# Turning the second attention group's queries by a transposing transfer in a two-layer encoder, and the keys' split at normal priority

## The chip, the cores and the metric

The kernel runs on one core of a Trainium2 chip, in one launch. The metric is the device time of the launch in microseconds. A core has a matrix engine (TensorE, PE in the profile, with its weight loads as PEld), VectorE (DVE), ScalarE (ACT), GpSimd (POOL) and SyncE (SP), whose queue here issues nearly all transfers. Every engine works through its own instructions in order and waits on semaphores for the others.

## The reference

Two layers of an encoder on 256 tokens with width 1024. Each layer normalizes its input, multiplies it by one wide matrix, feeds two branches with the parts, merges them, and goes on to a feed-forward part and an input embedding. The change lies in branch B, the attention: 8 query heads of 128, in two groups of 4, each group with one key and value head.

```python
u = rms_norm(h, g_mix_pre)
(gq, gk, gv, gg, ra_f, ra_b, aq, ak, av, gate_a, gate_b) = jnp.split(u @ w_in, offsets, axis=-1)
...
q = apply_axial_rope(rms_norm(aq.reshape(b, s, ATTN_HEADS, HEAD_DIM), g_q_norm), cos, sin)
k = apply_axial_rope(rms_norm(ak.reshape(b, s, ATTN_KV_HEADS, HEAD_DIM), g_k_norm), cos, sin)
v = av.reshape(b, s, ATTN_KV_HEADS, HEAD_DIM)
branch_b = gqa_attention(q, k, v) @ w_o_attn
...
sc = jnp.einsum('bqkgd,bskd->bkgqs', qblk, k).astype(jnp.float32) * scale
pr = jax.nn.softmax(sc, axis=-1).astype(v.dtype)
return jnp.einsum('bkgqs,bskd->bqkgd', pr, v)
```

Branch A is a gated linear attention, whose decays are built from the Abs, Exp and Ln of a projection.

## The kernel before

The 256 tokens are two halves of 128, one token in each partition. Every f32 product is made of three passes over rounded parts: each operand is split into a high part (rounded to fp32r) and a low part (the rest). `split(hi, lo, src)` does it with a cast on ACT (`nc.scalar.copy`) and a subtract on DVE, both on one line, L135 in the profile of before. Weights come by the SP queue into tiles named raw, ACT casts them to wh, DVE subtracts to wl, on the same line.

Names in the profile carry the layer and the stage: `acc_0v` is a PSUM accumulator of layer 0 in the projection of the gated branch's values, `aux_0at` a PSUM tile of the attention, `mid_0at` an on-chip tile of it, `big_0kv` the tile with the split keys and values, `mid_0rq` the rotated queries, `gqk`, `v`, `gg` the later projections, `gla` the gated branch. `acc` and `aux` share the 8 banks of PSUM, so that an accumulator can have to wait for the reader of the tile that had its bank before.

The projections are the main program. The attention and the gated branch are side tasks (`Task`), which a tick between groups of matmuls advances by a step; the `yield W[...]` say how many ticks each step waits. In this way the keys and the first group (g = 0) run in the projections kv and gqk, and the second group (g = 1) in v and gg. The build's scheduler orders each engine's instructions by priority: `tc.high_priority(n)` lets instructions go ahead of n others, and `tc.issue_after(x)` keeps them behind instruction x.

In `attend(g)`, for each half, PE turns the group's 4 heads of queries by 4 transposes (L1269) into an aux tile, and `split` takes them from there, at high priority in the first group alone. `softmax` makes the scores (matmuls on L107, `aux_0at<-big_0kv,mid_0at`), the maxima (L1230) and the exponentials (L1239); the last of these is kept in `last_exp`. `turn_p` turns the probabilities by PE (L1256) and splits them, and `passes` (L123) multiplies them by the values. `keys` turns the keys by PE (L1206) and splits them at L1209. `decays` is the gated branch's step with Abs, Exp and Ln (L1326 to L1328), read by DVE on L1329.

The kernel already has another way to turn a tile, used in the feed-forward part and for the out-gate: `turn_out` copies the f32 tile on ACT into two planes of 16-bit words (L467) and issues a transposing transfer (`dma_start_transpose`, L468) on the SP queue, and `take_in` has ACT put the turned planes together (L477) and splits the result.

Of the kernel before, what the change touches and what calls it, by code (L numbers as in the profile page):

```python
# [13 lines left out]
U16 = mybir.dt.uint16  # L14
# [4 lines left out]
P = 128  # L19
# [6 lines left out]
AHEAD, EMPTY, EMPTY_FIRST = 400, 100, 1600  # L26

WAIT, WAIT_FIRST = 6, 4

WAIT_NEXT, WAIT_IN, WAIT_H = (7, 9), ((6, 9), (6, 7)), ((3, 5), (3, 5))  # L30
WAIT_MIX = 3, 6
# [30 lines left out]
def trunk_kernel(ctx: ExitStack, tc: tile.TileContext, a: dict, out: bass.AP):  # L62
# [7 lines left out]
    nc = tc.nc  # L70
# [13 lines left out]
    def nm(s):  # L84
        uid[0] += 1
        return f"{s}_{part[0]}_{uid[0]}"
# [4 lines left out]
    def mid(dt=F32):  # L91
        return b4p.tile([P, 1024], dt, tag="mid", name=nm("mid"))
# [4 lines left out]
    def aux():  # L97
        return accp.tile([P, 512], F32, tag="acc", name=nm("aux"))

    def t512():  # L100
        return smp.tile([P, 512], F32, tag="t512", name=nm("t512"), bufs=5)

    def small(n, tag, bufs=None):
        return smp.tile([P, n], F32, tag=tag, name=nm(tag), **({"bufs": bufs} if bufs else {}))
# [10 lines left out]
    def passes(o, parts, start, stop, fresh=False, between=None, **kw):  # L115

        ps = [((xh, yh), (xh, yl), (xl, yh)) if fresh else ((xh, yh), (xl, yh), (xh, yl)) for (xh, xl), (yh, yl) in parts]  # L120
        seq = [p for t in ps for p in t[:2]] + [t[2] for t in ps]
        for n, (x, y) in enumerate(seq):
            nc.tensor.matmul(o, x, y, start=start and n == 0, stop=stop and n == len(seq) - 1, **kw)  # L123
            if between is not None and 2 * (n + 1) == len(seq):
                between()
# [7 lines left out]
    def split(hi, lo, src):  # L133

        return nc.scalar.copy(hi, src), nc.vector.tensor_tensor(out=lo, in0=src, in1=hi.bitcast(F32), op=ALU.subtract)  # L135
# [27 lines left out]
    ident = cp.tile([P, P], F32, tag="ident", name="ident")  # L163
# [204 lines left out]
    ws = Stream(4)  # L368
# [102 lines left out]
    def take_in(hi, lo, src, parts, behind=()):  # L471

        tn = hi.shape[-1]
        with ExitStack() as order:
            for x in behind:
                order.enter_context(tc.issue_after(x.ins))
            nc.scalar.copy(  # L477
                parts.bitcast(U16).rearrange("p (k t s) -> p k t s", s=2, t=tn),
                src.bitcast(U16).rearrange("p (s k t) -> p k t s", s=2, t=tn),
            )  # L480
            split(hi, lo, parts.rearrange("p (k t) -> p k t", t=tn))
# [7 lines left out]
    def inv_sqrt(t, n, mul, add, eps=None):  # L489

        with in_turn():
            if eps is None:
                nc.gpsimd.tensor_scalar(out=t, in0=t, scalar1=mul, scalar2=add, op0=ALU.mult, op1=ALU.add)
            else:
                nc.gpsimd.tensor_scalar(out=t, in0=t, scalar1=eps, scalar2=mul, op0=ALU.add, op1=ALU.mult)
        last_pow[0] = nc.gpsimd.tensor_tensor(out=t, in0=t, in1=neghalf[:, :n], op=ALU.pow)

    def split_by(hi, lo, src, r):

        nc.scalar.activation(hi, src, AF.Copy, bias=0.0, scale=r)  # L500
        nc.vector.scalar_tensor_tensor(
            out=lo, in0=src, scalar=r, in1=hi.bitcast(F32), op0=ALU.mult, op1=ALU.subtract
        )
# [43 lines left out]
    def halves(t):  # L547
        return [t[:, j * 512 : (j + 1) * 512] for j in range(2)]
# [501 lines left out]
    for l in range(DEPTH):  # L1050
# [11 lines left out]
        def rope(src, n, tabs, hf, dst):  # L1062

            ct, sn = tabs
            t2 = t512()
            hv = lambda t: t[:, : n * P].rearrange("p (h d) -> p h d", d=P)
            vmul(hv(dst), hv(src), ct[:, hf, :].unsqueeze(1).broadcast_to([P, n, P]))

            quad = lambda t: t.rearrange("p h (x y i) -> p h x y i", x=2, y=2)
            vmul(  # L1070
                quad(hv(t2)),
                quad(hv(src))[:, :, :, ::-1, :],
                quad(sn[:, hf, :].unsqueeze(1)).broadcast_to([P, n, 2, 2, 32]),
            )
            nc.vector.tensor_tensor(out=hv(dst), in0=hv(dst), in1=hv(t2), op=ALU.add)

        def head_ss(src, n, junk, ss):
            for i in range(n):
                s = slice(i * P, (i + 1) * P)
                nc.scalar.activation(junk[:, s], src[:, s], AF.Square, accum_out=ss[:, i : i + 1])  # L1080
# [28 lines left out]
        qrs, qss, ranks = [], [], []  # L1109
# [69 lines left out]
        kTh, kTl, avh, avl = (kv4[:, i * 512 : (i + 1) * 512] for i in range(4))  # L1179

        def keys(o):
            krs = []
            for hf in range(2):
                with tc.high_priority(EMPTY):
                    kr = t512()
                    ss = small(2, "kss")
                    head_ss(o[hf], 2, kr, ss)
                    inv_sqrt(ss, 2, 1.0 / P, EPS, eps[hf])
                    rope(o[hf], 2, ropes[1], hf, kr)
                    s = slice(hf * 256, (hf + 1) * 256)  # L1190
                    split_by(avh[:, s], avl[:, s], o[hf][:, 256:512], rows[hf])
                    for i in range(2):
                        s = slice(i * P, (i + 1) * P)
                        if l == 0:
                            nc.scalar.activation(kr[:, s], kr[:, s], AF.Copy, bias=0.0, scale=ss[:, i : i + 1])
                            continue
                        nc.vector.tensor_scalar(
                            out=kr[:, s], in0=kr[:, s], scalar1=ss[:, i : i + 1], scalar2=None, op0=ALU.mult
                        )
                krs.append(kr)  # L1200
            for hf in range(2):
                yield W["k"]
                ps = aux()
                for i in range(2):
                    s = slice(i * P, (i + 1) * P)
                    nc.tensor.transpose(ps[:, s], krs[hf][:, s], ident)  # L1206
                kv = lambda t: t.rearrange("p (g t) -> p g t", t=T)[:, :, hf * P : (hf + 1) * P]
                with tc.high_priority(AHEAD):
                    split(kv(kTh), kv(kTl), ps[:, 0:256].rearrange("p (g t) -> p g t", t=P))  # L1209

        keys = Task(keys(project(uT)), f"{l}kv")
        even = small(512, "rope0", 1)[:, 0:P]
        Task(spread(rho, even), f"{l}kv")
# [4 lines left out]
        last_exp = [None]  # L1218
# [32 lines left out]
        def turn_p(pr_):  # L1251
            res = []
            for s in range(2):
                ps = aux()
                for i in range(4):
                    nc.tensor.transpose(ps[:, i * P : (i + 1) * P], pr_[:, i, s * P : (s + 1) * P], ident)  # L1256
                pT = halves(mid(F32R))
                split(pT[0], pT[1], ps)
                res.append(pT)
            return res  # L1260

        def attend(g):
            qs = []
            for hf in range(2):
                yield W["q"]
                ps = aux()
                for i in range(4):
                    hd = 4 * g + i
                    nc.tensor.transpose(ps[:, i * P : (i + 1) * P], qrs[hf][:, hd * P : (hd + 1) * P], ident)  # L1269
                qh, ql = halves(mid(F32R))  # L1270
                with nullcontext() if g else tc.high_priority(AHEAD):
                    split(qh, ql, ps)
                qs.append((qh, ql, qss[hf][:, 4 * g : 4 * g + 4]))
            keys.need()
            yield W["a0"]
            prs = []
            for hf in range(2):
                prs.append(softmax(g, hf, qs[hf]))
                yield W["a1"]
            for hf in range(2):  # L1280
                pT = turn_p(prs[hf])
                yield W["a2"]
                o = aux()
                vs = [slice(s * 256 + g * P, s * 256 + (g + 1) * P) for s in range(2)]
                passes(o, [((avh[:, c], avl[:, c]), pT[s]) for s, c in enumerate(vs)], True, True)
                aT.put(o, 4 * g, 4, hf * P, P)
                yield W["a3"]

        def attention():
            for g_ in range(2):  # L1290
                part[0] = f"{l}at{g_}"
                yield from attend(g_)
# [500 lines left out]
```

## Time and profile before

| | |
|---|---|
| median of 3 runs | 905.2 us (905.08 to 906.77) |
| the profiled execution | 904.09 us |
| its span | 902.4 us |
| PE busy | 893.1 us (99%) |
| DVE busy | 789.8 us (88%) |
| ACT busy | 633.6 us (70%) |
| POOL busy | 98.1 us (11%) |

The profile is of one execution, and times in it count from the start of the span. A row of the timeline gives the start, the duration of a group of like instructions, their number (x4), and in brackets the idle time of the engine before them with what ended it. Durations of neighbours overlap a little, since an instruction begins before the one ahead of it is written out; from start to start is what one costs its engine. A row of the waits gives the sum, the number of times and the longest.

### The profile page before, as it was taken

How to read it: one execution, taken by the hardware profiler on the slowest of the kernel's cores; microseconds unless marked ns; L12 is line 12 of the kernel's file. 1: busy time of each engine (PE TensorE's matmuls, PEld its weight loads, DVE VectorE, ACT ScalarE, POOL GpSimd, SP SyncE). 2: the span in 40 equal slices, each digit the busy share in tenths (PEclk: the TensorE clock that was granted, in tenths of full speed). 3: DMA queues.
4: the chain of work that ended last, by engine and by line, in shares of the span. 5: the costliest groups of instructions: out<-in, count | busy, mean ns of one | idle time of the engine just before them, and what ended most of it. 6: DMA issues, size and time to landing. Idle time of an engine off the chain costs nothing.

```text
span 902.4 us, 12151 instructions
## 1 busy us (share of the span) xinstructions
PE 893.1 (99%) x4447; PEld 760.2 (84%) x4447; DVE 789.8 (88%) x1021; ACT 633.6 (70%) x1027; POOL 98.1 (11%) x157
## 2 busy tenths in 40 slices
PE   9999999999999999999999999999999999999996
PEld 8888888888888888888898888888888888888886
DVE  7889979997669989999779799799975799999984
ACT  6678769864468787766676687698645787867653
POOL 3700211000210000000334001110001100000001
PEclk9999999999999999999999999999999999999999
DMA  8754448369296785947476424474682966757441
GB/s 284 262 192 140 141 141 230 122 224 345 67 330 190 208 268 175 292 167 270 159 270 211 163 94 141 140 232 133 222 299 82 318 185 228 248 184 259 153 174 47
DMA packets 116967, 180.25 MB, mean 200 GB/s; under 512 B 30942, under 2 KB 55014, under 8 KB 116396
## 3 DMA queue, kind: packets, MB, share of 16 engines
q1 hardware_dynamic: 116748, 179.35, 59.7%
q8 instruction: 35, 0.57, 0.3%
q14 instruction: 24, 0.20, 0.1%
q10 hardware_dynamic: 160, 0.14, 0.0%
HBM read 169.50 MB, written 3.15 MB: 191 GB/s over the span
## 4 chain that ended last, share of the span: by engine, by line
PE 98%; issue 1%; ACT 0%; DVE 0%; POOL 0%; POOLq 0%
PE acc_1ffnin L123 12%; PE acc_0ffnin L123 12%; PE acc_1gate L123 7%; PE acc_0gate L123 7%; PE acc_1ffnin L107 7%; PE acc_0ffnin L107 7%; PE acc_1rq L123 3%; PE acc_1gqk L107 2%; PE acc_0v L123 2%; PE acc_0wout L123 2%; PE acc_1wout L123 2%; PE acc_0ple L123 2%; PE acc_0gg L123 2%; PE acc_1gg L123 2%; PE acc_1v L123 2%; PE acc_1merge L123 2%
## 5 line engine op out<-in xcount | busy, mean ns | idle before, releaser
L135 ACT CAST wh_1ffnin<-raw_1ffnin 128x1024 fp32r<-128x1024 f32 x38 | 38.6, 1050 | 20.6 <-PE acc_1ffnin L107 10.4
L135 ACT CAST wh_0ffnin<-raw_0ffnin 128x1024 fp32r<-128x1024 f32 x38 | 38.5, 1048 | 19.3 <-PE acc_0ffnin L107 9.6
L135 DVE TENSOR_TENSOR wl_0ffnin<-raw_0ffnin,wh_0ffnin 128x1024 fp32r<-128x1024 f32 x38 | 44.8, 1218 | 4.1 <-ACT wh_0ffnin L135 4.1
L135 DVE TENSOR_TENSOR wl_1ffnin<-raw_1ffnin,wh_1ffnin 128x1024 fp32r<-128x1024 f32 x38 | 45.0, 1219 | 3.3 <-ACT wh_1ffnin L135 3.1
L107 PE MATMUL acc_0ffnin<-wh_0ffnin,big_0ffnin 128*128 128x512 f32 x176 | 45.1, 390 | 0.0
L107 PE MATMUL acc_1ffnin<-wh_1ffnin,big_1ffnin 128*128 128x512 f32 x176 | 45.1, 390 | 0.0
L123 PE MATMUL acc_1ffnin<-wh_1ffnin,big_1wout 128*128 128x512 f32 x168 | 41.5, 389 | 0.0
L123 PE MATMUL acc_0ffnin<-wh_0ffnin,big_0wout 128*128 128x512 f32 x168 | 41.5, 389 | 0.0
L107 PEld LDWEIGHTS acc_1ffnin<-wh_1ffnin,big_1ffnin 128*128 128x128 f32 x176 | 33.0, 188 | 6.9
L107 PEld LDWEIGHTS acc_0ffnin<-wh_0ffnin,big_0ffnin 128*128 128x128 f32 x176 | 33.0, 188 | 6.9
L123 PEld LDWEIGHTS acc_1ffnin<-wh_1ffnin,big_1wout 128*128 128x128 f32 x168 | 31.5, 188 | 6.6
L123 PEld LDWEIGHTS acc_0ffnin<-wh_0ffnin,big_0wout 128*128 128x128 f32 x168 | 31.5, 188 | 6.5
L135 DVE TENSOR_TENSOR wl_1ffnin<-lent_1ffnin,wh_1ffnin 128x1024 fp32r<-128x1024 f32 x30 | 35.6, 1218 | 0.7 <-ACT wh_1ffnin L135 0.7
L135 DVE TENSOR_TENSOR wl_0ffnin<-lent_0ffnin,wh_0ffnin 128x1024 fp32r<-128x1024 f32 x30 | 35.6, 1218 | 0.3 <-ACT wh_0ffnin L135 0.3
L135 ACT CAST wh_1ffnin<-lent_1ffnin 128x1024 fp32r<-128x1024 f32 x30 | 30.4, 1050 | 4.9 <-DVE wl_1ffnin L135 2.8
L135 ACT CAST wh_0ffnin<-lent_0ffnin 128x1024 fp32r<-128x1024 f32 x30 | 30.4, 1053 | 4.2 <-DVE wl_0ffnin L135 2.5
L135 DVE TENSOR_TENSOR wl_1gate<-raw_1gate,wh_1gate 128x1024 fp32r<-128x1024 f32 x20 | 23.6, 1220 | 1.4 <-ACT wh_1gate L135 1.3
L135 DVE TENSOR_TENSOR wl_0gate<-raw_0gate,wh_0gate 128x1024 fp32r<-128x1024 f32 x20 | 23.6, 1220 | 1.4 <-ACT wh_0gate L135 1.3
L135 ACT CAST wh_1gate<-raw_1gate 128x1024 fp32r<-128x1024 f32 x20 | 20.1, 1051 | 5.7 <-PE acc_1gate L123 5.6
L135 ACT CAST wh_0gate<-raw_0gate 128x1024 fp32r<-128x1024 f32 x20 | 20.1, 1052 | 5.7 <-PE acc_0gate L123 5.5
L107 PE MATMUL acc_1ffnin<-wl_1ffnin,big_1ffnin 128*128 128x512 f32 x88 | 24.1, 391 | 0.0
L107 PE MATMUL acc_0ffnin<-wl_0ffnin,big_0ffnin 128*128 128x512 f32 x88 | 24.1, 391 | 0.0
(730 smaller groups left out, 2736.9 us busy)
## 6 DMA issues: line engine op xcount, KB each, us to landing
raw_0ffnin<-in_w_ffn_out_dram SPq DMA_DIRECT2D x11, 1024.0 KB, 5.2
raw_1ffnin<-in_w_ffn_out_dram SPq DMA_DIRECT2D x11, 1024.0 KB, 6.1
lent_0ffnin<-in_w_ffn_in_dram SPq DMA_DIRECT2D x6, 1024.0 KB, 5.0
lent_1ffnin<-in_w_ffn_in_dram SPq DMA_DIRECT2D x6, 1024.0 KB, 7.6
raw_0v<-in_w_in_dram SPq DMA_DIRECT2D x4, 1024.0 KB, 4.9
raw_0gate<-in_w_o_gla_dram SPq DMA_DIRECT2D x4, 1024.0 KB, 5.1
raw_0gate<-in_w_o_attn_dram SPq DMA_DIRECT2D x4, 1024.0 KB, 5.3
raw_0wout<-in_w_ffn_in_dram SPq DMA_DIRECT2D x8, 512.0 KB, 4.3
```

Source lines behind the costliest of these rows:

```text
L107: return nc.tensor.matmul(o, lhsT, rhs, start=start, stop=stop)
L123: nc.tensor.matmul(o, x, y, start=start and n == 0, stop=stop and n == len(seq) - 1, **kw)
L135: return nc.scalar.copy(hi, src), nc.vector.tensor_tensor(out=lo, in0=src, in1=hi.bitcast(F32), op=ALU.subtract)
```

## The change

First, in `keys`, the split of the turned keys loses its high priority. Second, the second group's queries are turned without PE. When the first group's probabilities of a half have been turned, `turn_q_out(hf)` lets ACT copy the second group's 4 heads of that half, as two planes of 16-bit words, into the place of the first group's heads (which have been read), behind the last exponential, and a transposing transfer on the SP queue brings them back turned. Third, `attend(1)` has `take_in` put them together on ACT, and splits them from there.

```diff
                 kv = lambda t: t.rearrange("p (g t) -> p g t", t=T)[:, :, hf * P : (hf + 1) * P]
-                with tc.high_priority(AHEAD):
-                    split(kv(kTh), kv(kTl), ps[:, 0:256].rearrange("p (g t) -> p g t", t=P))
+                split(kv(kTh), kv(kTl), ps[:, 0:256].rearrange("p (g t) -> p g t", t=P))
...
+        def turn_q_out(hf):
+            t, src = halves(qrs[hf])
+            with tc.issue_after(last_exp[0].ins):
+                nc.scalar.copy(
+                    t.bitcast(U16).rearrange("p (z c) -> p z c", z=2), src.bitcast(U16).rearrange("p (c z) -> p z c", z=2)
+                )
+            nc.sync.dma_start_transpose(out=src.bitcast(U16).rearrange("p (x t) -> p x t", t=P), in_=t.bitcast(U16))
+
         def attend(g):
             qs = []
             for hf in range(2):
                 yield W["q"]
-                ps = aux()
-                for i in range(4):
-                    hd = 4 * g + i
-                    nc.tensor.transpose(ps[:, i * P : (i + 1) * P], qrs[hf][:, hd * P : (hd + 1) * P], ident)
                 qh, ql = halves(mid(F32R))
-                with nullcontext() if g else tc.high_priority(AHEAD):
-                    split(qh, ql, ps)
+                if g:
+                    t, src = halves(qrs[hf])
+                    take_in(*(x.rearrange("p (k t) -> p k t", t=P) for x in (qh, ql)), src, t, ws.cast)
+                else:
+                    ps = aux()
+                    for hd in range(4):
+                        nc.tensor.transpose(ps[:, hd * P : (hd + 1) * P], qrs[hf][:, hd * P : (hd + 1) * P], ident)
+                    with tc.high_priority(AHEAD):
+                        split(qh, ql, ps)
...
                 yield W["a2"]
+                if g == 0:
+                    turn_q_out(hf)
                 o = aux()
```

Lines after the first few of the file are one higher in the changed kernel, and those behind the new function 13 higher.

The first place is DVE in layer 0, in the projection kv, where the keys are split; `big_0kv<-aux_0kv` are the two halves of the keys, `mid_0at` the first group's queries of the second half, `wl_0kv` weights. Before:

```order
L135 TENSOR_TENSOR wl_0kv_571<-raw_0rq_423,wh_0kv_570 128x1024
L135 TENSOR_TENSOR big_0kv_539<-aux_0kv_684,big_0kv_539 128x2x128
L135 TENSOR_TENSOR mid_0at_710<-aux_0at_705,mid_0at_710 128x512
L135 TENSOR_TENSOR big_0kv_539<-aux_0kv_713,big_0kv_539 128x2x128
L135 TENSOR_TENSOR wl_0kv_603<-raw_0rq_528,wh_0kv_602 128x1024 x2
L1230 TENSOR_REDUCE mx_0at_734<-aux_0at_727 128x2
```

And in the changed kernel:

```order
L136 TENSOR_TENSOR wl_0kv_571<-raw_0rq_423,wh_0kv_570 128x1024
L136 TENSOR_TENSOR mid_0at_705<-aux_0at_706,mid_0at_705 128x512
L136 TENSOR_TENSOR wl_0kv_603<-raw_0rq_528,wh_0kv_602 128x1024 x2
L136 TENSOR_TENSOR big_0kv_539<-aux_0kv_684,big_0kv_539 128x2x128
L136 TENSOR_TENSOR big_0kv_539<-aux_0kv_713,big_0kv_539 128x2x128
L136 TENSOR_TENSOR wl_0gqk_768<-raw_0kv_576,wh_0gqk_767 128x1024
```

Both halves of the keys have moved behind the queries' split and behind two weight subtracts.

The second place is ACT in layer 0, at the end of the projection gqk; `mid_0at` are the first group's turned probabilities, `big_0gqk` the projection's results, `mid_0gla` the first decays. Before:

```order
L135 CAST mid_0at_892<-aux_0at_887 128x512
L135 CAST mid_0at_900<-aux_0at_895 128x512
L1305 ACTIVATE big_0gqk_639<-acc_0gqk_784 128x256
L1305 ACTIVATE big_0gqk_639<-acc_0gqk_785 128x256
L1305 ACTIVATE big_0gqk_639<-acc_0gqk_786 128x256
L1326 ACTIVATE mid_0gla_933<-aux_0gla_930 128x512
```

And in the changed kernel:

```order
L136 CAST mid_0at_892<-aux_0at_887 128x512
L136 CAST mid_0at_900<-aux_0at_895 128x512
L1318 ACTIVATE big_0gqk_639<-acc_0gqk_785 128x256
L1265 COPY mid_0rq_161<-mid_0rq_161 128x1024
L1318 ACTIVATE big_0gqk_639<-acc_0gqk_786 128x256
L1339 ACTIVATE mid_0gla_933<-aux_0gla_930 128x512
```

The first half's copy apart (L1265) now stands ahead of the last evacuation and of the decays' Abs.

The third place is PE in layer 0, in the projection v, up to the second group's first scores. Before:

```order
L1269 MATMUL aux_0at_1166<-ident,mid_0rq_161 128x128 x4
L123 MATMUL acc_0v_1121<-wh_0v_1026,big_start_303 128x512 x6
...
L123 MATMUL acc_0v_1122<-wh_0v_1026,big_start_303 128x512 x6
L1269 MATMUL aux_0at_1217<-ident,mid_0rq_163 128x128 x4
L123 MATMUL acc_0v_1122<-wh_0v_1026,big_start_303 128x512 x2
L123 MATMUL acc_0v_1122<-wl_0v_1027,big_start_303 128x512 x4
L107 MATMUL aux_0at_1232<-big_0kv_539,mid_0at_1171 128x256 x6
```

And in the changed kernel:

```order
L124 MATMUL acc_0v_1126<-wl_0gqk_912,big_start_149 128x512 x4
L124 MATMUL acc_0v_1125<-wh_0v_1028,big_start_303 128x512 x6
...
L124 MATMUL acc_0v_1126<-wh_0v_1028,big_start_303 128x512 x8
L124 MATMUL acc_0v_1126<-wl_0v_1029,big_start_303 128x512 x4
L108 MATMUL aux_0at_1228<-big_0kv_539,mid_0at_1170 128x256 x6
```

The two groups of four transposes from `mid_0rq` are gone, and the second group's scores follow the projection's matmuls directly. Layer 1 loses its two groups in the same way.

## The prediction

> **What bounds the kernel now.** I read the page first, then the waits of TensorE (PE), then windows around the two stages that the change touches, then the timelines of PE, VectorE (DVE) and ScalarE (ACT) there.
>
> ```profile
> PE 893.1 (99%) x4447; PEld 760.2 (84%) x4447; DVE 789.8 (88%) x1021; ACT 633.6 (70%) x1027; POOL 98.1 (11%) x157
> PE 98%; issue 1%; ACT 0%; DVE 0%; POOL 0%; POOLq 0%
> PE acc_0v L123 <- DVE mid_0at L135: 1.2, 1, 1.2
> PE warm L107 <- POOL seed L144: 1.0, 1, 1.0
> 70.00:105.00 35.00, 33.84 (x178) 28.75 (x177) 34.94 (x61) 27.96 (x56) 5.61 (x4) 1.00 0.34 113
> 521.00:556.00 35.00, 35.00 (x186) 29.85 (x185) 33.92 (x56) 27.93 (x57) 4.48 (x4) 1.00 0.33 112
> ```
>
> PE is busy 99% of the span and makes up 98% of the chain of waits, so the time is PE's work plus what PE waits. It waits twice: 1.0 us at the start, and 1.2 us for DVE in layer 0. The two windows (length; then PE, weight loads, DVE, ACT, POOL) hold the second half of the attention in layer 0 and layer 1. There DVE is busy 34.94 and 33.92 of 35 us: it is as full as PE, and ACT has 7 us free. Hence two rules for the sum: what leaves PE counts one for one, and what makes DVE late in these windows stays late, until it eats the slack of a PE matmul. The granted clock is 1.00 in both.
>
> **Four groups of transposes leave PE.**
>
> ```profile
> 93.22 0.60 PE L1269 MATMUL aux_0at<-ident,mid_0rq 128*128 128x128 f32 x4
> 93.58 1.64 PE L123 MATMUL acc_0v<-wh_0v,big_start 128*128 128x512 f32 x6
> 95.05 0.60 PE L107 MATMUL aux_0gla<-t_0gla,mid_0gla 128*128 128x128 f32 x4
> 97.76 1.53 PE L123 MATMUL acc_0v<-wh_0v,big_start 128*128 128x512 f32 x6
> 99.13 0.60 PE L1269 MATMUL aux_0at<-ident,mid_0rq 128*128 128x128 f32 x4
> 99.48 0.71 PE L123 MATMUL acc_0v<-wh_0v,big_start 128*128 128x512 f32 x2
> 100.03 1.09 PE L123 MATMUL acc_0v<-wl_0v,big_start 128*128 128x512 f32 x4
> 100.95 1.60 PE L107 MATMUL aux_0at<-big_0kv,mid_0at 128*128 128x256 f32 x12
> ```
>
> Ends overlap, so a group's cost is from its start to the next start. The four transposes take 99.48 − 99.13 = 0.35. The matmuls behind them also run slower: six take 1.47 behind transposes (93.58 to 95.05) and 1.37 elsewhere (97.76 to 99.13); two take 0.55 (99.48 to 100.03), a third of 1.37 being 0.46. That is 0.10 more. So one group costs 0.455 us, two are gone in each of two layers: 4 × 0.455 = **−1.82 us**.
>
> The Trainium skill, VectorE: DVE Perf Modes, § The three transpose paths, lists 390 ns for a 128×128 bf16 transpose on TensorE and 1309 ns through the DMA crossbar; by an estimate from it 16 would give back 6.2 us. The rows (0.455 us for four f32 ones in a row) decide for 1.82.
>
> **What takes their place** is measured in the same kernel, where other tiles are turned in this way:
>
> ```profile
> L467 ACT COPY mid_0ffnin<-t_0ffnin x6: 1041/1046/1047, 266.8 to 372.4; 128x1024 uint16<-128x1024 uint16 x6
> L468 SPq DMA_TRANSPOSE mid_0gg<-big_0gg x4: 1247/1334/1869, 147.4 to 152.2; - x4
> DMA to landing us min/median/max: 3.1/3.5/4.1
> L477 ACT COPY mid_0ffnin<-t_0ffnin x9: 1163/1172/1185, 280.2 to 382.0; 128x1024 uint16<-128x1024 uint16 x9
> 85.82 0.37 SPq L298 DMA_DIRECT2D raw_0v<-in_w_in_dram  x1
> 75.67 0.20 ACT L1344 ACTIVATE eq_0gla<-mid_0gla 128x2 f32<-128x2 f32 x1
> 88.12 0.20 ACT L1344 ACTIVATE eq_0gla<-mid_0gla 128x2 f32<-128x2 f32 x1 [0.34 <-DVE mid_0gla L1335]
> 92.83 2.00 ACT L135 CAST wh_0v<-raw_0v 128x1024 fp32r<-128x1024 f32 x2
> ```
>
> Per half, ACT gets a copy of 1.04 us (planes apart) and later one of 1.17 (planes together): 4.4 us in each layer, into a window with 7 us free. The ACT cast and DVE subtract of the split stay, only their source is now on-chip memory instead of PSUM; the added DVE work is none. The transfers themselves are off the path. The first copy runs ahead of the Ln that is quoted next (72.48), the second behind the eq at 75.67; each transfer lands at most 4.1 us after its issue, so both are home by about 83, also where a copy comes 2 us late. The copies that read them stand in ACT's order behind the eq at 88.12 and the weight casts at 92.83. In the SyncE queue the two transfers stand behind the first load of raw_0v and ahead of the second, which was issued at 85.82: about 6 us of room, so nothing behind is held. GpSimd's queue does not change.
>
> **ACT's first copy makes DVE late in layer 0.** It stands between the casts of the turned probabilities and the decays' Abs, Exp, Ln.
>
> ```profile
> 72.48 1.22 ACT L1328 ACTIVATE mid_0gla<-mid_0gla 128x512 f32<-128x512 f32 x2
> 71.75 1.41 DVE L1306 SCALAR_TENSOR_TENSOR big_0gqk<-acc_0gqk,big_0gqk 128x256 f32<-128x256 f32 x4
> 73.22 1.29 DVE L1329 SCALAR_TENSOR_TENSOR mid_0gla<-aux_0gla,mid_0gla 128x512 f32<-128x512 f32 x2
> 98.91 0.68 DVE L135 TENSOR_TENSOR mid_0at<-aux_0at,mid_0at 128x512 fp32r<-128x512 f32 x1
> ```
>
> Before, DVE's L1329 began as the first Ln ended (72.48 + 0.6) and its own queue came free (73.16): both at once. With 1.04 us more on ACT, 0.1 of it overlapped, DVE waits about 0.9, and with 34.94 of 35 us busy it does not catch up. The second copy and the ones that take in stand where ACT waits for DVE or casts weights far ahead; I cost them at nothing, and that cover is the weakest point: the other bound is that all three copies ahead of the half's split pass on, 1.04 + 1.04 + 1.17 = 3.25.
>
> The reader that feels it is the second group's first score. The low part of its queries is done at 98.91 + 0.68 = 99.59, and the third matmul of the x12 group is the first to read it: 100.95 + 2 × 0.12 = 101.19. Slack 1.6. PE comes 0.91 sooner by two groups of transposes and 0.2 by the keys (below), which leaves 0.5. Late by 0.9: **+0.4 us**.
>
> **In layer 1** the same goes with other margins:
>
> ```profile
> 524.63 1.29 DVE L1329 SCALAR_TENSOR_TENSOR mid_1gla<-aux_1gla,mid_1gla 128x512 f32<-128x512 f32 x2 [0.98 <-ACT mid_1gla L1328]
> 520.73 1.05 ACT L135 CAST wh_1v<-raw_1gqk 128x1024 fp32r<-128x1024 f32 x1 [0.28 <-PE acc_1gqk L107]
> 549.18 0.68 DVE L135 TENSOR_TENSOR mid_1at<-aux_1at,mid_1at 128x512 fp32r<-128x512 f32 x1
> 551.09 1.59 PE L107 MATMUL aux_1at<-big_1kv,mid_1at 128*128 128x256 f32 x12
> ```
>
> ACT had 0.28 idle, so its Ln and DVE's L1329 come 0.95 − 0.28 = 0.7 later. Slack at the score: 551.33 − 549.86 = 1.47, less 0.91 for the transposes: 0.56. Late by 0.7: **+0.1 us**.
>
> **The keys' split.** In layer 1 its place among DVE's rows is the same: nothing. In layer 0 it falls behind the queries' split and two weight subtracts.
>
> ```profile
> 51.73 0.59 ACT L135 CAST mid_0at<-aux_0at 128x512 fp32r<-128x512 f32 x1 [0.55 <-PE aux_0at L1269]
> 51.03 1.21 DVE L135 TENSOR_TENSOR wl_0kv<-raw_0rq,wh_0kv 128x1024 fp32r<-128x1024 f32 x1
> 52.90 0.42 DVE L135 TENSOR_TENSOR big_0kv<-aux_0kv,big_0kv 128x256 fp32r<-128x256 f32 x1 [0.66 <-ACT big_0kv L135]
> 53.24 0.68 DVE L135 TENSOR_TENSOR mid_0at<-aux_0at,mid_0at 128x512 fp32r<-128x512 f32 x1
> 53.84 0.41 DVE L135 TENSOR_TENSOR big_0kv<-aux_0kv,big_0kv 128x256 fp32r<-128x256 f32 x1
> 54.17 2.35 DVE L135 TENSOR_TENSOR wl_0kv<-raw_0rq,wh_0kv 128x1024 fp32r<-128x1024 f32 x2
> 54.68 0.40 PE L107 MATMUL acc_0gqk<-big_start,wh_0kv 128*128 128x512 f32 x1
> 54.91 1.35 PE L107 MATMUL aux_0at<-big_0kv,mid_0at 128*128 128x256 f32 x10
> 71.29 1.88 PE L123 MATMUL acc_0v<-wh_0gqk,big_start 128*128 128x512 f32 x7 [1.16 <-DVE mid_0at L135]
> 70.55 1.28 DVE L135 TENSOR_TENSOR mid_0at<-aux_0at,mid_0at 128x512 fp32r<-128x512 f32 x2
> ```
>
> Now DVE starts the queries' split at 52.32 (the cast's end), is through at 52.92, subtracts the weights until 55.2 (2.27 from start to start), and the first half of the keys' split ends at 55.6. PE's acc_0gqk takes the PSUM bank of those turned keys and stood at 54.68: a wait of about **+0.95 us** on DVE's big_0kv. Queued behind it on PE are the score's x10 and everything else.
>
> In return, the 0.66 us for which DVE sat idle before the keys' split is used, so DVE runs that much ahead. The wait at acc_0v was 1.16 us, for the first of the two subtracts at 70.55. PE now arrives 0.95 later, and the subtract is 0.66 sooner, together more than 1.16: **−1.16 us**. Net of the keys' part: −0.2. Bounds: if casts or score rows keep the subtract where it was, PE still waits 0.2, net 0; if PE's wait near 54.7 is half as long, −0.2 all the same, because what PE does not wait there it waits at acc_0v.
>
> **Sum**: −1.82 + 0.95 − 1.16 + 0.4 + 0.1 = −1.5 us. The profiled run took 904.09 with a span of 902.4; it would take 902.6. The median of the three runs is 1.1 above the profiled run (905.2), so the median becomes 903.7. A difference of 0.2%, about what a measurement of this kernel can tell from no change, is 1.8 us: 903.4 to 907.0.
>
> **Rivals.**
> *Nothing is given back* (the copies find idle ACT time, or the DVE rows that changed places absorb them): −1.82 − 0.2 = −2.0, median 903.2, down to 902.7 if DVE also gains elsewhere. For it: ACT has 7 us free in each window. Against: the Ln and DVE's queue met at 73.2 with no slack.
> *The keys' wait stays whole*: the wait at acc_0v is not shortened since both PE and DVE shift with it: −1.82 + 0.95 + 0.5 = −0.4, median 904.8. Against: DVE's own order there no longer waits for the keys' cast.
> *Slower, by DVE's lateness at the second group's score.* All three ACT copies ahead of the split pass on, 3.25 us in each layer: PE waits 3.25 − 0.5 and 3.25 − 0.56, together 5.4, and the sum is 5.4 − 2.0 = +3.4, median 908.6. It cancels the gain from about 1.5 us of lateness in each layer and is slower by 0.2% from about 2.4. For it: DVE is full in both windows, and what one ACT copy delays, DVE cannot recover. Against: of the copies only the first stands directly ahead of work that DVE waits for. The Trainium skill, VectorE: DVE Perf Modes, § Rules for kernel authors, says to transpose 128×128 on TensorE if PSUM will do, and to take the crossbar otherwise; it would side with this rival.
> *The transfers are late* (a queue held, a transfer that waits for the second copy until 86): the second raw_0v load comes later and the take-in copy stalls ACT; same sign and place as the last, a small share.
>
> **How the numbers follow.** Forecast 0.45, with its own range 903.2 to 904.3; nothing given back 0.20; the keys' wait whole 0.15; slower 0.17; late transfers 0.03. About a third of the forecast's share lies beyond −1.8. Faster: 0.20 + 0.14 = 0.34. Same: 0.31 + 0.15 = 0.46. Slower: 0.20. The range runs from 902.7 (the gaining rival's end) to 907.2, the nearer part of the slower rival; beyond it lie some 0.05 below and 0.13 above.
>
> **What would show it.** In the changed profile: no second group of transposes from mid_0rq; a PE wait of about 1 us at acc_0gqk near 54.7 on DVE big_0kv, and none at acc_0v near 71; a wait of some tenths at aux_0at near 100 on DVE mid_0at, and near nothing in layer 1; copies of 1.04 and 1.17, transfers that land within 4.1 us. It is wrong if PE waits for DVE by more than 1 us at the second group's scores, or if a new PE wait stands on a weight tile.

## The result, and the profile after

The changed kernel takes 904.21 us (median of 22 runs, 903.24 to 906.26) beside 905.3 us for the kernel before in the same sessions (22 runs, 904.28 to 907.22): 1.1 us less, a ratio of 0.9986 with a 95% interval of 0.998 to 0.9992. The interval leaves out 1, so it is faster, by less than 0.2%; the forecast was -1.5 us.

The page of the changed kernel, then its waits of PE (engine, line, what was waited for, sum, times, longest):

```profile
PE 892.9 (99%) x4431; PEld 759.0 (84%) x4431; DVE 790.0 (87%) x1021; ACT 641.4 (71%) x1035; POOL 104.4 (12%) x157
PE warm L108 <- POOL seed L145: 1.0, 1, 1.0
PE acc_0gqk L108 <- DVE big_0kv L136: 0.9, 1, 0.9
PE aux_0at L108 <- DVE mid_0at L136: 0.6, 1, 0.6
```

PE has 16 matmuls fewer, ACT 8 instructions and 8 us more. The wait at acc_0v is gone, one of 0.9 us at acc_0gqk has come, and a third, of 0.6 us, at the second group's scores.

The profiled run of the changed kernel has a span of 903.0 us, longer than the 902.4 of before, although its median is shorter. Spans of single runs cannot show this change: the projection kv began 0.75 us later, and the feed-forward part, where no row differs, took 0.2 and 0.3 us more in the two layers. So I read the starts of stages on PE's timeline. These rows bound the stretches that differ, before (with acc_0v at 71.29, as quoted in the prediction) and in the changed kernel:

```profile
41.73 1.07 PE L107 MATMUL acc_0gqk<-big_start,wh_0rq 128*128 128x512 f32 x4
102.39 2.00 PE L123 MATMUL acc_0gg<-wh_0v,big_start 128*128 128x512 f32 x8
521.49 2.00 PE L123 MATMUL acc_1v<-wh_1gqk,big_0ple 128*128 128x512 f32 x8
552.51 2.00 PE L123 MATMUL acc_1gg<-wh_1v,big_0ple 128*128 128x512 f32 x8
```

```profile
42.48 1.07 PE L108 MATMUL acc_0gqk<-big_start,wh_0rq 128*128 128x512 f32 x4
71.84 2.00 PE L124 MATMUL acc_0v<-wh_0gqk,big_start 128*128 128x512 f32 x8
102.87 2.00 PE L124 MATMUL acc_0gg<-wh_0v,big_start 128*128 128x512 f32 x8
522.14 2.00 PE L124 MATMUL acc_1v<-wh_1gqk,big_0ple 128*128 128x512 f32 x8
552.59 2.00 PE L124 MATMUL acc_1gg<-wh_1v,big_0ple 128*128 128x512 f32 x8
```

From one start to the next, in us, with the kernels of the experiments:

| kernel | layer 0, acc_0gqk to acc_0v | layer 0, acc_0v to acc_0gg | layer 1, acc_1v to acc_1gg | sum against before | medians against before in the same session |
|---|---|---|---|---|---|
| before | 29.56 | 31.10 | 31.02 | | |
| changed | 29.36 | 31.03 | 30.45 | -0.84 | -1.1 |
| keys_only | 29.37 | 31.08 | 31.03 | -0.20 | -0.5 |
| transfer_only | 29.59 | 30.16 | 30.44 | -1.49 | -1.3 |
| after_ln | 29.36 | 30.15 | 30.08 | -2.09 | -1.7 |
| transfer_ln | 29.58 | 30.17 | 30.08 | -1.85 | -1.7 |
| twice | 29.37 | 31.04 | 31.32 | +0.05 | 0.0 |
| pool | 31.08 | 30.27 | 30.09 | -0.24 | -0.5 |
| transfer_ln_p | 29.06 | 30.17 | 30.08 | -2.37 | -2.2 |

In all nine profiles, kernels with the same rows in a stretch agree in it within 0.04 us, and the projection kv in front takes 11.25 or 11.26 in each. The ratios' intervals are 0.5 us wide to each side for the changed kernel and 0.8 to 0.9 for the others, and a ratio is not the quotient of the two medians (in pool the medians differ by -0.5 us, the ratio is 1.0001). The stretches are the finer measure, and within these intervals the two agree.

The places of the forecast, on PE in layer 0 of the changed kernel:

```profile
56.48 0.73 PE L108 MATMUL acc_0gqk<-big_start,wh_0kv 128*128 128x512 f32 x2 [0.88 <-DVE big_0kv L136]
97.84 1.98 PE L124 MATMUL acc_0v<-wh_0v,big_start 128*128 128x512 f32 x8
99.66 1.07 PE L124 MATMUL acc_0v<-wl_0v,big_start 128*128 128x512 f32 x4
100.56 0.40 PE L108 MATMUL aux_0at<-big_0kv,mid_0at 128*128 128x256 f32 x2
101.58 1.46 PE L108 MATMUL aux_0at<-big_0kv,mid_0at 128*128 128x256 f32 x10 [0.62 <-DVE mid_0at L136]
```

and in layer 1, the first row from before and the others from the changed kernel:

```profile
535.17 1.53 PE L123 MATMUL aux_1at<-mid_1at,big_1kv 128*128 128x512 f32 x6
535.82 1.88 PE L124 MATMUL aux_1at<-mid_1at,big_1kv 128*128 128x512 f32 x6
551.16 1.60 PE L108 MATMUL aux_1at<-big_1kv,mid_1at 128*128 128x256 f32 x12
```

The projection's matmuls now run on without transposes between them; the scores start, and after two matmuls (the ones that read the queries' high part) PE stands for their low part. In layer 1 there is no wait at the scores, but the six matmuls by the values take 1.88 instead of 1.53: a wait of 0.35 that lies within a group and is named nowhere in the list of waits. It is one for DVE: the last of the six starts at 537.20, where DVE's second subtract of these probabilities ends at 537.15 (a row of two that starts at 535.87 and takes 1.28; before, it started at 534.75, 0.42 ahead of PE's group).

What was added cost what it costs elsewhere in the kernel:

```profile
L1265 ACT COPY mid_0rq<-mid_0rq x2: 1031/1066/1100, 71.2 to 77.7; 128x1024 uint16<-128x1024 uint16 x2
L478 ACT COPY mid_0rq<-mid_0rq x2: 1147/1165/1183, 90.2 to 97.2; 128x1024 uint16<-128x1024 uint16 x2
L1268 SPq DMA_TRANSPOSE mid_0rq<-mid_0rq x2: 1238/1293/1348, 72.3 to 78.8; - x2
DMA to landing us min/median/max: 4.6/4.6/4.6
```

The profile has the landing of the first transfer alone: 4.6 us after its issue, where 3.1 to 4.1 was expected. If the second takes as long, it is home at 83.4 (an estimate), and the copies that read them start at 90.2 and 97.2: off the path, as forecast.

### The profile page after: what moved, and what is told of

It is laid out like the page before. It is cut to its first block, busy times and chain, and to the rows that moved or that the text cites. A ratio compares the mean times of both kernels' runs of the same rounds, so it can differ in the third digit from the quotient of the medians.

```text
span 903.0 us, 12130 instructions
## 1 busy us (share of the span) xinstructions
PE 892.9 (99%) x4431; PEld 759.0 (84%) x4431; DVE 790.0 (87%) x1021; ACT 641.4 (71%) x1035; POOL 104.4 (12%) x157
## 3 DMA queue, kind: packets, MB, share of 16 engines
HBM read 169.50 MB, written 3.15 MB: 191 GB/s over the span
## 4 chain that ended last, share of the span: by engine, by line
PE 87%; DVE 6%; ACT 3%; issue 2%; DMA 1%; POOL 0%; POOLq 0%; ACTq 0%
PE acc_0ffnin L124 12%; PE acc_1ffnin L124 10%; PE acc_1gate L124 7%; PE acc_0gate L124 7%; PE acc_0ffnin L108 7%; PE acc_1ffnin L108 5%; PE acc_1rq L124 3%; PE acc_0wout L124 2%; PE acc_1wout L124 2%; PE acc_0ple L124 2%; PE acc_0gg L124 2%; PE acc_1gg L124 2%; PE acc_1merge L124 2%; PE acc_0merge L124 2%; PE acc_1ple L124 2%
```

## The experiments

The question was where 1.0 us of the 1.82 that the transposes gave back went: what makes the second group's queries late, the copies as such or their place, and what the keys' split has to do with it.

**keys_only**: the kernel before with the first hunk of the change alone.

```diff
-                with tc.high_priority(AHEAD):
-                    split(kv(kTh), kv(kTl), ps[:, 0:256].rearrange("p (g t) -> p g t", t=P))
+                split(kv(kTh), kv(kTl), ps[:, 0:256].rearrange("p (g t) -> p g t", t=P))
```

> The kernel before with the keys' split at normal priority and nothing else. Read from PE's timeline: from the first acc_0gqk to the first acc_0v it was 29.56 us before and 29.36 after; from there to the first acc_0gg 31.10 and 31.03. Theory (the wait only changes its place): PE waits 0.9 at acc_0gqk on DVE's big_0kv and not at acc_0v, 29.36 for the first stretch; the second 31.1, since the second group's queries have 1.6 us of slack and the late turned probabilities cost 0.5 of them; time -0.2 us. Rival (the wait at acc_0v stays, and in the changed kernel something else took it away): first stretch 30.0 or more, time +0.5.

904.36 us beside 904.87, ratio 0.9997 (0.9988 to 1.0006); stretches 29.37, 31.08, 31.03. The theory held in the stretches (the whole times cannot tell this run from before): the keys' split alone is a trade of waits worth -0.2. Its wait of PE in layer 0, then the start of its stage, and ACT and DVE ahead of the decays' first step (L1328 here):

```profile
PE acc_0gqk L107 <- DVE big_0kv L135: 0.9, 1, 0.9
```

```profile
43.53 1.07 PE L107 MATMUL acc_0gqk<-big_start,wh_0rq 128*128 128x512 f32 x4
72.26 1.10 ACT L135 CAST wh_0v<-raw_0gqk 128x1024 fp32r<-128x1024 f32 x1
74.31 1.22 DVE L135 TENSOR_TENSOR wl_0v<-raw_0gqk,wh_0v 128x1024 fp32r<-128x1024 f32 x1
76.21 1.29 DVE L1328 SCALAR_TENSOR_TENSOR mid_0gla<-aux_0gla,mid_0gla 128x512 f32<-128x512 f32 x2 [0.68 <-ACT mid_0gla L1327]
```

DVE takes that step 32.68 us after the stage's start, where it was 31.49 before (73.22 - 41.73): the delay is there without any copy, and PE does not feel it.

**transfer_only**: the changed kernel with the keys' split back at high priority.

```diff
-                split(kv(kTh), kv(kTl), ps[:, 0:256].rearrange("p (g t) -> p g t", t=P))
+                with tc.high_priority(AHEAD):
+                    split(kv(kTh), kv(kTl), ps[:, 0:256].rearrange("p (g t) -> p g t", t=P))
```

> The changed kernel with the keys' split back at high priority. In layer 0 the scheduler then puts ACT's first copy behind the decays' Ln; in layer 1 the order is that of the changed kernel. Theory (the second group's wait in layer 0 comes from the first copy's place ahead of the Abs, and from the keys' wait, which has PE late by 0.9 between 55 and 71): first stretch 29.56 as before, second 30.2 with a wait under 0.2 at aux_0at; layer 1 from the first acc_1v to the first acc_1gg 30.45 as in the changed kernel (before 31.02); time -1.5 us. Rival (any 3.3 us of copies ahead of the split on ACT make it late, wherever they stand): second stretch 31.0 again, time -0.6.

903.61 us beside 904.87, ratio 0.9983 (0.9973 to 0.9992); stretches 29.59, 30.16, 30.44. All three fall on the theory. The second stretch gives back the whole of two groups of transposes (31.10 - 30.16 = 0.94, by the forecast 0.91), with the same four copies per layer on ACT. So in layer 0, where the first copy now starts at 73.3, behind the Ln, copies as such cost nothing, and the two parts of the change work against each other: -0.20 and -1.49 apart, -0.84 together. PE's waits in layer 0, as before the change:

```profile
PE acc_0v L124 <- DVE mid_0at L136: 1.2, 1, 1.2
```

**after_ln**: the changed kernel with the copies apart issued after the first decays' second Ln, in both layers.

```diff
-        last_exp = [None]
+        last_exp, last_ln = [None], []
...
-            with tc.issue_after(last_exp[0].ins):
+            with tc.issue_after((last_ln[1] if len(last_ln) > 1 else last_exp[0]).ins):
...
-                nc.scalar.activation(t0, t0, AF.Ln, bias=1.0)
+                last_ln.append(nc.scalar.activation(t0, t0, AF.Ln, bias=1.0))
```

> The changed kernel with ACT's copies apart held behind the first decays' Ln, in both layers; keys' split at normal priority. Theory (place of the first copy): DVE's L1342 is late in layer 0 by the keys' 0.5 alone, not by 0.95 more: first stretch 29.36, second 30.2 to 30.4 with a wait of 0 to 0.2 at aux_0at; layer 1 30.1, without the hidden wait of 0.35 at aux_1at; time -1.8 us. Rival (copies anywhere): second stretch 31.0, layer 1 30.45, time -0.8 as the changed kernel by the same count.

903.19 us beside 904.87, ratio 0.9987 (0.9978 to 0.9997); stretches 29.36, 30.15, 30.08. The place of the first copy is thus what cost 0.88 in layer 0 (31.03 against 30.15) and 0.37 in layer 1. How it cost that in layer 0 is not what the theory said. ACT around the first copy in the changed kernel:

```profile
70.92 0.44 ACT L1318 ACTIVATE big_0gqk<-acc_0gqk 128x256 f32<-128x256 f32 x1
71.20 1.10 ACT L1265 COPY mid_0rq<-mid_0rq 128x1024 uint16<-128x1024 uint16 x1
72.13 0.45 ACT L1318 ACTIVATE big_0gqk<-acc_0gqk 128x256 f32<-128x256 f32 x1
74.41 1.23 ACT L1341 ACTIVATE mid_0gla<-mid_0gla 128x512 f32<-128x512 f32 x2
```

and in after_ln, with the row from which its times count (42.23, 0.25 us earlier than in the changed kernel):

```profile
42.23 1.07 PE L108 MATMUL acc_0gqk<-big_start,wh_0rq 128*128 128x512 f32 x4
70.68 0.45 ACT L1318 ACTIVATE big_0gqk<-acc_0gqk 128x256 f32<-128x256 f32 x1
70.95 1.10 ACT L136 CAST wh_0v<-raw_0gqk 128x1024 fp32r<-128x1024 f32 x1
71.89 0.45 ACT L1318 ACTIVATE big_0gqk<-acc_0gqk 128x256 f32<-128x256 f32 x1
74.17 1.23 ACT L1341 ACTIVATE mid_0gla<-mid_0gla 128x512 f32<-128x512 f32 x2
```

The gap that the copy left was filled by a weight cast of the same length, so the Ln came no sooner. DVE in the changed kernel, then in after_ln:

```profile
71.93 1.41 DVE L1319 SCALAR_TENSOR_TENSOR big_0gqk<-acc_0gqk,big_0gqk 128x256 f32<-128x256 f32 x4
75.15 1.29 DVE L1342 SCALAR_TENSOR_TENSOR mid_0gla<-aux_0gla,mid_0gla 128x512 f32<-128x512 f32 x2 [1.82 <-ACT mid_0gla L1341]
100.84 0.68 DVE L136 TENSOR_TENSOR mid_0at<-mid_0rq,mid_0at 128x512 fp32r<-128x512 f32 x1
```

```profile
71.69 1.41 DVE L1319 SCALAR_TENSOR_TENSOR big_0gqk<-acc_0gqk,big_0gqk 128x256 f32<-128x256 f32 x4
73.01 1.22 DVE L136 TENSOR_TENSOR wl_0v<-raw_0gqk,wh_0v 128x1024 fp32r<-128x1024 f32 x1
74.91 1.29 DVE L1342 SCALAR_TENSOR_TENSOR mid_0gla<-aux_0gla,mid_0gla 128x512 f32<-128x512 f32 x2 [0.68 <-ACT mid_0gla L1341]
99.64 0.68 DVE L136 TENSOR_TENSOR mid_0at<-mid_0rq,mid_0at 128x512 fp32r<-128x512 f32 x1
```

In both, DVE takes the decays' first step (L1342) at the same time after the stage's start (75.15 - 42.48 = 32.67 and 74.91 - 42.23 = 32.68), and that is also the time of keys_only. What differs is what it does until then: with the cast in the gap it has a weight subtract to do (1.22 us) and is idle for 0.68; with the copy in the gap it is idle for 1.82. The subtract left undone has to be done later, ahead of the second group's split, which starts 0.95 later (58.36 and 57.41 after the stage's start), although ACT's cast of the same queries starts at the same time in both (94.77 - 42.48 = 52.29 and 94.53 - 42.23 = 52.30). That is the cost of the copy beside the keys' change: 1.14 us of DVE's time in a stage in which DVE is full, and not the lateness of the Ln. No run leaves ACT's gap empty, so it is not shown whether the Ln would come sooner with neither copy nor cast in it: PE's last matmuls of the projection end at 71.5 in the changed kernel, and the last evacuation starts at 72.13, so at most 0.6 (an estimate).

In layer 1 the copy does delay the Ln. ACT has both the copy and the weight cast ahead of it there, and DVE still has its subtract in the gap:

```profile
522.93 1.23 DVE L136 TENSOR_TENSOR wl_1v<-raw_1gqk,wh_1v 128x1024 fp32r<-128x1024 f32 x1
525.00 1.23 ACT L1341 ACTIVATE mid_1gla<-mid_1gla 128x512 f32<-128x512 f32 x2
```

Counted from the first acc_1v, the Ln starts at 2.86 (525.00 - 522.14), where it is 2.47 before and 2.48 in after_ln; DVE takes the decays' step at 3.61, where it is 3.14 and 3.15. This lateness of 0.47 is what the products with the values wait for.

**transfer_ln**: both, the keys' split at high priority and the copies behind the Ln.

> Both: keys' split at high priority and the copies apart behind the first decays' Ln in both layers. Theory: first stretch 29.56, second 30.2, layer 1 30.1; time -1.8 us, which is what the four groups of transposes cost PE. Rival (copies anywhere): -0.6.

903.16 us beside 904.87, ratio 0.9982 (0.9974 to 0.9991); stretches 29.58, 30.17, 30.08: -1.85, which is the price of the four groups of transposes as the prediction had it.

**twice**: the changed kernel, with the first half's copy apart made twice.

```diff
-                nc.scalar.copy(
+                for _ in range(1 if hf else 2):
+                    nc.scalar.copy(
```

> The changed kernel with the first half's copy apart made twice in each layer (same data, about 1 us more on ACT). In layer 0 the extra copy stands behind the first decays' Ln and the rows of DVE, PE and SP are the same; in layer 1 it stands between the casts of the turned probabilities and the Abs. Theory (only what stands ahead of Abs, Exp, Ln makes DVE late): layer 0, first acc_0v to first acc_0gg, 31.03 to 31.2 (31.03 in the changed kernel); layer 1, first acc_1v to first acc_1gg, 30.45 + 0.95 less what is left of slack, 31.0 to 31.4, with named waits on DVE; time +0.5 to +1.1 us over the changed kernel. Rival (any copy ahead of the split counts): layer 0 goes to 31.9 as well, time +1.7 or more.

905.15 us beside 905.14, ratio 1.0002 (0.9993 to 1.0011); stretches 29.37, 31.04, 31.32. In layer 0, where the extra copy stands behind the Ln, a microsecond more on ACT costs nothing: the rival that any copy counts is out. In layer 1, where it stands ahead, the stretch is 0.87 longer, and now the wait at the scores is there too. DVE's decays there in the changed kernel, then the stage's start, ACT's Ln, DVE's decays and PE's wait in this one:

```profile
525.75 1.29 DVE L1342 SCALAR_TENSOR_TENSOR mid_1gla<-aux_1gla,mid_1gla 128x512 f32<-128x512 f32 x2 [1.26 <-ACT mid_1gla L1341]
```

```profile
521.51 2.00 PE L124 MATMUL acc_1v<-wh_1gqk,big_0ple 128*128 128x512 f32 x8
524.36 1.23 ACT L1342 ACTIVATE mid_1gla<-mid_1gla 128x512 f32<-128x512 f32 x2
525.11 1.29 DVE L1343 SCALAR_TENSOR_TENSOR mid_1gla<-aux_1gla,mid_1gla 128x512 f32<-128x512 f32 x2 [2.11 <-ACT mid_1gla L1342]
551.54 1.46 PE L108 MATMUL aux_1at<-big_1kv,mid_1at 128*128 128x256 f32 x10 [0.62 <-DVE mid_1at L136]
```

DVE's idle time was 1.26 in the changed kernel and 0.98 before; 2.11 here. But the Ln comes no later: it starts 2.85 after the stage's start and DVE takes the step at 3.60, where both were the same in the changed kernel (2.86 and 3.61). The second copy stands at 521.14, in the place where the changed kernel casts a weight (521.78), and the subtract that DVE made at 522.93 there is missing from the gap. DVE makes it later, and the second group's split starts 1.13 later (550.79 - 521.51 = 29.28 against 550.29 - 522.14 = 28.15). So this is the same cost as in layer 0, a weight cast pushed out of a gap: 1.13 us of lateness on DVE, 0.87 on PE.

**pool**: the changed kernel with the copies apart on GpSimd.

```diff
-                nc.scalar.copy(
+                nc.gpsimd.tensor_copy(
                     t.bitcast(U16).rearrange("p (z c) -> p z c", z=2), src.bitcast(U16).rearrange("p (c z) -> p z c", z=2)
                 )
```

> The changed kernel with the copies apart on GpSimd instead of ACT. Theory: ACT's Abs, Exp, Ln are not delayed, so layer 0's second stretch is 30.2 and layer 1 30.1, first stretch 29.4, time -2 us against the kernel before, if GpSimd needs less than some 8 us for a copy; its transfers now stand ahead of a weight load on the SP queue, which is issued 14 us or more before its cast. Rival: GpSimd's copy takes so long, or slows DVE beside it so much, that the second group comes late: second stretch over 31.

904.65 us beside 905.14, ratio 1.0001 (0.9991 to 1.0011); stretches 31.08, 30.27, 30.09. The second and third came as the theory had them. The first is 1.7 longer than in the changed kernel, which neither theory had: a miss. The copies ran at 46.5 and 51.6 instead of 71 and 78, and took their transfers along, which then stood in the SP queue ahead of weight loads and waited there for copies that waited for the first group's transposes:

```profile
L1265 POOL COPY mid_0rq<-mid_0rq x2: 1039/1208/1376, 46.5 to 51.6; 128x1024 uint16<-128x1024 uint16 x2
L1268 SPq DMA_TRANSPOSE mid_0rq<-mid_0rq x2: 1237/1288/1339, 47.5 to 53.0; - x2
59.79 2.00 ACT L136 CAST wh_0gqk<-raw_0kv 128x1024 fp32r<-128x1024 f32 x2 [3.15 <-DMA raw_0kv<-in_w_in_dram]
62.92 0.17 DVE L1243 RECIPROCAL sm_0at<-sm_0at 128x2 f32<-128x2 f32 x1 [2.38 <-ACT mid_0at L1239]
```

ACT stood 3.15 us for a load of raw_0kv, the exponentials behind it came late, DVE was idle for 2.38, and PE waited for DVE once more at acc_0v. The expectation had counted 14 us from the load behind the transfers to its cast; for the second load of raw_0kv it is 4.9 in the changed kernel (53.07 to 58.01), so there was nothing to spare: the load is issued 2.2 later after the stage's start, and its cast starts 2.7 later. `issue_after` had held the copy behind the last exponential in ACT's queue; on GpSimd's it did not.

**transfer_ln_p**: transfer_ln, and the first half's turned probabilities (first group, layer 0) split at high priority.

```diff
-                split(pT[0], pT[1], ps)
+                with tc.high_priority(AHEAD) if first else nullcontext():
+                    split(pT[0], pT[1], ps)
...
-                pT = turn_p(prs[hf])
+                pT = turn_p(prs[hf], l + g + hf == 0)
```

> Keys' split at high priority, the copies apart behind the first decays' Ln in both layers, and the first half's turned probabilities of the first group in layer 0 split at high priority, which puts their subtract on DVE ahead of a pair of scalings (0.53 us). Theory: PE's wait of 1.17 us at acc_0v becomes 0.6; first stretch 29.0, second 30.2, layer 1 30.1; time -2.4 us against the kernel before. Rival (the scalings come later, and with them the second half's probabilities): the 0.5 comes back at aux_0at behind, second stretch 30.7, time -1.9.

902.97 us beside 905.14, ratio 0.9977 (0.9969 to 0.9986); stretches 29.06, 30.17, 30.08. By the stretches this is the fastest of the kernels here, 2.4 us under the kernel before and about 1.5 under the changed one (its ratio's interval overlaps those of after_ln and transfer_ln). The wait that it was aimed at went from 1.17 to 0.65, and nothing of that came back behind:

```profile
PE acc_0v L124 <- DVE mid_0at L136: 0.7, 1, 0.7
```

## Why the prediction was right, and where it was not

The forecast, -1.5 us and 903.7, had the sign right, and also what PE gains and the trade of waits; 904.21 lies in its range, and within 0.2% of before, as the likeliest case had it. The two terms that bring time back were both too small, 0.5 forecast and 1.25 measured, so that by the stretches little more than half of the forecast gain is left. That the median came within 0.5 of the forecast is in part luck of the medians, which say -1.1. Term by term, in the stretches:

- Transposes, -1.82: right. Without a wait behind them the two layers give 0.94 (transfer_only) and 0.94 (after_ln), -1.88 in all.
- The keys' split, +0.95 and -1.16, net -0.2: right, with a wait of 0.88 at acc_0gqk on DVE's big_0kv, none at acc_0v, and -0.20 in the stretch.
- What comes back in layer 0, +0.4: the term that was mis-sized. It is 0.88. The step was "ACT's first copy makes DVE late": 0.9 us were priced as a delay of the Ln. But DVE takes the decays' first step as late in keys_only (32.68 us after the stage's start), where there is no copy, as in the changed kernel (32.67). So the delay comes with the keys' part: PE, held 0.88 at acc_0gqk, starts its last matmuls of the projection 1.1 later (70.90 - 42.48 = 28.42, before 69.02 - 41.73 = 27.29), and in ACT's gap ahead of the last evacuation stands the copy or, without one, a weight cast. What the copy does is push out a weight cast, whose subtract would have filled DVE's gap. The second group's split is then 1.18 later than before (58.36 against 98.91 - 41.73 = 57.18), which the slack of 0.5 at the scores turns into 0.7. PE loses 0.88 there: the third matmul of the scores starts 1.01 after the first instead of 0.23 (the wait of 0.62 is the idle part of that), and it takes 0.22 instead of 0.12 to the next one.
- What comes back in layer 1, +0.1: 0.37, at a place that the sum had not looked at. The mechanism was the forecast one, a later Ln, and smaller: DVE is 0.47 late where 0.7 was forecast. The slack at the scores held (no wait there), but the products with the values of the first group, for which the sum had no slack worked out, waited 0.35 us inside a group of six.
- Transfers, POOL and SP at nothing: right for the changed kernel, though the one landing that was measured took 4.6 us, over the 4.1 that the prediction named as a sign. The pool run shows what the SP queue costs when that cover is gone: 1.7 us.

Sum by the stretches -1.88 - 0.20 + 0.88 + 0.37 = -0.83. The rule that was weighed, the Trainium skill's advice to transpose on TensorE if PSUM will do (VectorE: DVE Perf Modes, § Rules for kernel authors), does not decide here: with PE busy 99% and the transfers hidden, the crossbar's way gave 1.85 us in transfer_ln. The estimate of 6.2 from the Trainium skill's 390 ns for one bf16 transpose (the same page, § The three transpose paths) was too high by more than three times: four f32 ones in a row cost 0.455.

Left open: the changed kernel's medians say -1.1 and the stretches -0.84, which the intervals cover. Three things were not tried: whether an empty gap on ACT would bring the Ln sooner, what the copy ahead of the Ln would cost in layer 0 without the keys' change, and why the start and the feed-forward part differ by some tenths between runs of the same rows.

## What to carry to other kernels

Where two engines are full side by side, price an instruction on the third by the work that it pushes out of a gap as well as by its own delay: here a copy of 1 us cost 0.9 us in layer 0 because the cast that would have fed the full engine came after it, 0.4 in layer 1 where it delayed the Ln, and nothing a few rows later. Check the slack of every reader of the engine that comes late, not only of the one that you expect to feel it. Two edits that each gain can take from one another, if one moves a wait forward and so opens the gap into which the other falls (here -0.20 and -1.49 apart, -0.84 together): run them apart before keeping both. For effects of a tenth of a percent, compare the starts of stages in the traces: they agreed to 0.04 us here, where whole runs of one kernel spread over about 3.

## What the runs showed that was not expected

A wait of 0.35 us between matmuls of one group is in no list of waits: it shows only as a group that takes 1.88 instead of 1.53. A GpSimd copy of 128x1024 words of 16 bits took 1.04 and 1.38 us in layer 0, not much longer than ACT's 1.03 and 1.10, so that moving it was not ruled out by its price but by the order that it took. In layer 0 of the changed kernel the first transposing transfer, issued 1.5 us behind a weight load (70.84 and 72.32), landed after 4.6 us; in the five kernels where it followed that load by 4.5 us or more, after 3.1. That the load made it slower was not tried apart.
